# Expert weights by table products: both one-hots from TensorE and ScalarE, shorter lookups on VectorE

## The chip, the cores and the metric

One core of a Trainium2 chip runs the whole kernel. The metric is the device time of one execution in microseconds (us); of several executions the median is given. The core's engines each have an in-order stream of instructions: TensorE (PE, its weight loads PEld), VectorE (DVE), ScalarE (ACT), GpSimd (POOL, which here issues gathers by index), SyncE (SP, which issues the other transfers).

## The reference

One layer of a hybrid encoder over 1024 tokens of width 1024: attention and a long convolution side by side, then a feed-forward part with product keys (PEER), which is where the change lies. For each token and each of 8 heads it finds the 16 best of 128 x 128 experts and sums what they say:

```python
s = jnp.einsum('chpd,hpnd->chpn', q, sub_keys)
sv, si = lax.top_k(s, PEER_TOPK)
cand = sv[:, :, 0, :, None] + sv[:, :, 1, None, :]
cidx = si[:, :, 0, :, None] * PEER_NKEYS + si[:, :, 1, None, :]
...
best, pos = lax.top_k(cand, PEER_TOPK)
eidx = jnp.take_along_axis(cidx, pos, axis=-1)
g = jax.nn.softmax(best, axis=-1)
u = u_tab[eidx]
a = jax.nn.gelu(jnp.einsum('chkd,cd->chk', u, xc), approximate=False)
vv = v_tab[eidx]
return jnp.einsum('chk,chkd->cd', (g * a).astype(vv.dtype), vv)
```

## The kernel before

The 1024 tokens are 8 tiles of 128. Three tiles (NG = 3) are done by gathers: for each of their 128 (head, rank) slots one indirect transfer brings the rows of `peer_u`, and one those of `peer_v`, into `grow` (six buffers), and VectorE takes the dot product (L1244) or adds the weighted row (L1252). The other five (DENSE = 5, 640 tokens) are done by matmuls over all 16384 experts in 128 blocks of 128: `u_part(i)` loads block i of `peer_u` into `ur` (512 KB, one buffer), splits it into a high part `uh` on ScalarE (L291) and a low part `ul` on VectorE (L292), multiplies both with the tokens in two halves of 320 columns (48 matmuls, L285 to L287, into the four banks of `ps_x`) and applies Gelu on ScalarE (L1204). Later the result is weighted with `gt`, the block's column of the table `g_d`, and multiplied with `peer_v`.

The table `g_d` holds for each dense token the weight of every expert; it is what the change makes in another way. For each tile `route` works on VectorE: the best 16 of 128 scores for 16 half-heads (L1019 to L1023), 50 candidate sums a head and their expert numbers (L1039), the best 16 of them (L1045 to L1049), then the look-up of the expert number for each rank: a comparison of the rank's position with 0 to 49, a product with the candidates' numbers, a sum (L1057, L1060, L1061), head by head, 16 ranks x 50 elements each. For a dense tile it then splits the number e into i = e >> 7 and j = e & 127, keeps i as a float, and writes j and j squared in two parts (`jx`) by way of DRAM (`jx_d`, L1093) into `jl` (three loads, L1096), ready to be a matmul's stationary operand. Two transposes on TensorE bring i and the weight w into `ig`.

`build_g` then goes through the tile's 128 tokens, four at a time (32 steps a tile, 160 in all). A step has

```python
nc.tensor.matmul(ps, jl[0:98, c // 32], par_r[0:98, c % 32:c % 32 + NB], start=True, stop=True)
...
nc.vector.tensor_tensor(p1, iota..., ig[:, 0, c:c + NB]..., op=ALU.is_equal)
...
nc.scalar.activation(p2[:, j], ps[:, j], AF.Relu, scale=ig[:, 1, c + j:c + j + 1])
...
nc.tensor.matmul(ps[:, j], p2[:, j], p1[:, j], start=True, stop=True)
```

The first line is a table product: it gives 1 - (j - n) squared for all n from 0 to 127, whose positive part is 1 where n = j and else 0. So `p2` is a one-hot of j, scaled by the weight, made on TensorE and ScalarE; `p1` is a one-hot of i, made by a comparison on VectorE (L1155). The last line multiplies the two for each token (four products), and ScalarE evicts them to `gst` (L1178), which SP writes to `g_d`. Table products run two steps ahead in the two banks of `ps_o`, the one-hots one step ahead.

Order: the first 72 expert blocks (EARLY) are written out beside routing and table building. `weights()` yields an estimated cost at each chunk of route (CHUNK, 14 chunks in all) and at each step of build_g (HOT), and after each 1/71 of the total one `u_part` is written; `tick` likewise paces the gathers. In `weights()` every second step of build_g is followed by one chunk of the next tile's route. From this order a list scheduler of the language lays down each engine's stream before the run, so an instruction can stand before others written ahead of it.

## Time and profile before

| | |
|---|---|
| median of 3 runs | 3322.92 us (3304.04 to 3323.4) |
| the profiled execution | 3313.74 us, span 3312.0 us, mean granted clock 0.958 |
| TensorE busy | 2999.0 us, 91% of the span |
| VectorE busy | 2782.6 us, 84% |
| ScalarE busy | 1254.5 us, 38% |
| GpSimd busy | 1052.3 us, 32% |
| bytes moved | 828.88 MB, mean 250 GB/s |

Busy time is time in which an engine has an instruction under way; matmuls overlap and their ends are modelled, so a busy TensorE isn't one at its peak. Shares are means over stages with different limits, so a change is read in its own stage. The granted clock is TensorE's; 1 is full speed.

### The profile page before, as it was taken

How to read it: one execution, taken by the hardware profiler on the slowest of the kernel's cores; microseconds unless marked ns; L12 is line 12 of the kernel's file. 1: busy time of each engine (PE TensorE's matmuls, PEld its weight loads, DVE VectorE, ACT ScalarE, POOL GpSimd, SP SyncE). 2: the span in 40 equal slices, each digit the busy share in tenths (PEclk: the TensorE clock that was granted, in tenths of full speed). 3: DMA queues.
4: the chain of work that ended last, by engine and by line, in shares of the span. 5: the costliest groups of instructions: out<-in, count | busy, mean ns of one | idle time of the engine just before them, and what ended most of it. 6: DMA issues, size and time to landing. Idle time of an engine off the chain costs nothing.

```text
span 3312.0 us, 44979 instructions
## 1 busy us (share of the span) xinstructions
PE 2999.0 (91%) x15582; PEld 2558.2 (77%) x15582; DVE 2782.6 (84%) x5610; ACT 1254.5 (38%) x2454; POOL 1052.3 (32%) x797
## 2 busy tenths in 40 slices
PE   6999888889999678888989979998999999899997
PEld 4676666655799677788878978886788888688886
DVE  7556899787747999899999978888788888888886
ACT  4544334556333114464555622222222222222222
POOL 0000000000000343334235445555555555555540
PEclk9999999989999899999999989999999999999998
DMA  5344743321454777778778899999899999999993
GB/s 171 103 147 149 236 117 99 99 71 51 160 174 147 259 271 247 267 284 301 273 257 320 327 309 344 331 348 342 310 341 335 354 325 322 346 347 346 330 338 111
DMA packets 355065, 828.88 MB, mean 250 GB/s; under 512 B 34345, under 2 KB 144851, under 8 KB 351253
## 3 DMA queue, kind: packets, MB, share of 16 engines
q1 hardware_dynamic: 243957, 422.25, 38.0%
q0 software_dynamic: 110592, 402.70, 33.9%
q8 instruction: 123, 2.02, 0.2%
q10 hardware_dynamic: 288, 1.05, 0.1%
q14 instruction: 105, 0.86, 0.1%
HBM read 715.52 MB, written 110.33 MB: 249 GB/s over the span
## 4 chain that ended last, share of the span: by engine, by line
PE 36%; DVE 15%; DMA 13%; issue 4%; ACT 2%; SPq 1%; POOL 1%; DVEq 0%; ACTq 0%; POOLq 0%
PE ps_x L285 6%; PE ps_x L287 6%; PE ps_x L286 6%; DMA vr<-in_peer_v 5%; DMA ur<-in_peer_uT 4%; DVE grow L1244 3%; PE ps_h L287 3%; PE ps_h L285 3%; PE ps_h L286 3%; PE ps_h L1177 3%; DVE gacc L1252 2%; PE ps_o L285 2%; PE ps_o L286 2%; PE ps_o L287 2%; DMA grow<-in_peer_u,eid 2%
## 5 line engine op out<-in xcount | busy, mean ns | idle before, releaser
L1231 POOL DMA_INDIRECT grow<-in_peer_v,eid x384 | 516.8, 1346 | 645.2 <-DVE gacc L1252 337.7
L1231 POOL DMA_INDIRECT grow<-in_peer_u,eid x384 | 522.0, 1359 | 560.7 <-DVE grow L1244 211.2
L1252 DVE SCALAR_TENSOR_TENSOR gacc<-grow,dot,gacc 128x1024 f32<-128x1024 f32 x381 | 487.3, 1279 | 6.9 <-DMA grow<-in_peer_v,eid 4.2
L1244 DVE SCALAR_TENSOR_TENSOR grow<-grow,gh 128x1024 f32<-128x1024 f32 x384 | 460.7, 1217 | 15.2 <-DMA grow<-in_peer_u,eid 15.0
L287 PE MATMUL ps_x<-hd,ul 128*128 128x320 f32 x1152 | 371.7, 331 | 54.7 <-DVE ul L292 54.4
L285 PE MATMUL ps_x<-hd,uh 128*128 128x320 f32 x1152 | 377.3, 328 | 39.0 <-ACT uh L291 38.9
L286 PE MATMUL ps_x<-hd,uh 128*128 128x320 f32 x1152 | 373.1, 325 | 0.0
L286 PE MATMUL ps_x<-vl,wh 128*128 128x512 f32 x864 | 341.5, 395 | 7.0 <-DVE vl L292 7.0
L287 PE MATMUL ps_x<-vh,wl 128*128 128x512 f32 x864 | 337.0, 393 | 0.0
L285 PE MATMUL ps_x<-vh,wh 128*128 128x512 f32 x864 | 306.4, 397 | 12.5 <-ACT vh L291 9.6
L291 ACT CAST vh<-vr 128x512 fp32r<-128x512 f32 x256 | 157.3, 619 | 414.8 <-DMA vr<-in_peer_v 304.7
L285 PE MATMUL ps_h<-hd,uh 128*128 128x320 f32 x896 | 279.5, 312 | 20.9 <-ACT uh L291 16.8
L287 PE MATMUL ps_h<-hd,ul 128*128 128x320 f32 x896 | 276.5, 312 | 2.7 <-DVE ul L292 2.6
L286 PE MATMUL ps_h<-hd,uh 128*128 128x320 f32 x896 | 278.6, 311 | 0.0
L287 PEld LDWEIGHTS ps_x<-hd,ul 128*128 128x128 f32 x1152 | 224.3, 197 | 67.8 <-DVE ul L292 62.9
L285 PEld LDWEIGHTS ps_x<-hd,uh 128*128 128x128 f32 x1152 | 227.4, 197 | 45.7 <-ACT uh L291 44.0
L291 ACT CAST uh<-ur 128x1024 fp32r<-128x1024 f32 x128 | 134.9, 1054 | 319.1 <-DMA ur<-in_peer_uT 231.3
L292 DVE TENSOR_TENSOR vl<-vr,vh 128x512 fp32r<-128x512 f32 x256 | 174.5, 686 | 94.8 <-ACT vh L291 94.6
L286 PEld LDWEIGHTS ps_x<-hd,uh 128*128 128x128 f32 x1152 | 227.2, 197 | 1.1
L285 PEld LDWEIGHTS ps_x<-vh,wh 128*128 128x128 f32 x864 | 163.2, 191 | 47.7 <-ACT vh L291 11.7
L1161 ACT ACTIVATE p<-ps_o,ig 128x128 f32<-128x128 f32 x640 | 185.4, 403 | 35.3 <-PE ps_o L1148 35.2
L286 PEld LDWEIGHTS ps_x<-vl,wh 128*128 128x128 f32 x864 | 164.8, 191 | 42.1 <-DVE vl L292 9.4
(363 smaller groups left out, 6904.3 us busy)
## 6 DMA issues: line engine op xcount, KB each, us to landing
ur<-in_peer_uT SPq DMA_DIRECT2D x128, 512.0 KB
vr<-in_peer_v SPq DMA_DIRECT2D x256, 256.0 KB
g_d<-gst SPq DMA_DIRECT2D x20, 2048.0 KB
gt<-g_d SPq DMA_DIRECT2D x32, 1280.0 KB
a_d<-A SPq DMA_DIRECT2D x72, 320.0 KB
A<-a_d SPq DMA_DIRECT2D x72, 320.0 KB
fw<-in_dft_fw SPq DMA_DIRECT2D x64, 256.0 KB
wr<-in_w_in SPq DMA_DIRECT2D x16, 512.0 KB
```

The lines of the kernel that those rows point to most:

```text
L285: nc.tensor.matmul(out, L[0], R[0], start=start, stop=False)
L286: nc.tensor.matmul(out, L[0], R[1], start=False, stop=False)
L287: nc.tensor.matmul(out, L[1], R[0], start=False, stop=stop)
L291: nc.scalar.copy(hi, src)
L292: return nc.vector.tensor_sub(lo, src, hi)
L1161: nc.scalar.activation(p2[:, j], ps[:, j], AF.Relu, scale=ig[:, 1, c + j:c + j + 1])
L1177: nc.tensor.matmul(ps[:, j], p2[:, j], p1[:, j], start=True, stop=True)
L1231: nc_i = nc.gpsimd.indirect_dma_start(out=t, out_offset=None, in_=a["peer_" + kind], in_offset=bass.IndirectOffsetOnAxis(ap=eid[g][:, k:k ...
L1244: nc.vector.scalar_tensor_tensor(t, t, 1.0, h_t, op0=ALU.mult, op1=ALU.mult, accum_out=d[:, k - k0:k - k0 + 1])
L1252: nc.vector.scalar_tensor_tensor(acc, t, dots[k0][:, k - k0:k - k0 + 1], acc, op0=ALU.mult, op1=ALU.add)
```

## The change

The one-hot of i is made as that of j is. `route` writes i, j and their squares, each square in two parts, as six rows (`xb`, through `x_d`) and loads them with six transfers into a `jl` with a slot for i and one for j; only the weight is still transposed. `parabola` does two table products a step, that for i into a bank of `ps_x`, that for j into `ps_o` as before; `hots` takes the positive part of the first with one activation over four tokens (128x512), in place of the comparison.

The candidates are put in another order, so that those that can have rank 0 to 3 are the first 16 and those that can have rank 4 to 7 are within the first 32. The look-up then goes by ranks: ranks 0 to 3 of all heads over 16 candidates, ranks 4 to 7 over 32, ranks 8 to 15 over 50 in two halves of the heads: four groups of three instructions with 512, 1024, 1600 and 1600 elements, where there were eight groups of 800. The constants of the order follow (12 chunks of route, three of five steps of build_g followed by one).

```diff
@@ -1003,10 +1003,14 @@
 
     NEG = -3.0e38
     NCAND = 50
-    rows = [(0, 1, 16), (1, 1, 8), (2, 1, 5), (3, 1, 4), (4, 1, 3), (5, 3, 2), (8, 8, 1)]
+    blocks = [(0, 4, 0, 4), (0, 2, 4, 4), (4, 4, 0, 2), (0, 1, 8, 8), (8, 8, 0, 1), (2, 1, 4, 1), (4, 1, 2, 1)]
+    finds = [(0, 8, 0, 4, 16), (0, 8, 4, 8, 32), (0, 4, 8, 16, NCAND), (4, 8, 8, 16, NCAND)]
 
     routed = []
-    CHUNK = 62.0 / 14
+    CHUNK = 55.0 / 12
 
     def route(tt, rp, done):
 
@@ -1032,10 +1036,10 @@
         nc.vector.tensor_scalar(sf4[:, :, 0], sf4[:, :, 0], 128.0, None, op0=ALU.mult)
         for eng, dst, src in ((nc.vector, cand, sv4), (nc.vector, cidx, sf4)):
             off = 0
-            for a0, na, nb in rows:
+            for a0, na, b0, nb in blocks:
                 o = dst[:, :, off:off + na * nb].rearrange("p h (x y) -> p h x y", y=nb)
                 x = src[:, :, 0, a0:a0 + na].unsqueeze(3).to_broadcast([P, 8, na, nb])
-                y = src[:, :, 1, 0:nb].unsqueeze(2).to_broadcast([P, 8, na, nb])
+                y = src[:, :, 1, b0:b0 + nb].unsqueeze(2).to_broadcast([P, 8, na, nb])
                 eng.tensor_add(o, x, y)
                 off += na * nb
             assert off == NCAND
@@ -1052,15 +1056,16 @@
         pf = rp.tile([P, 8, 16], F32, name="r_pf")
         nc.vector.tensor_copy(pf, pos)
         ef = rp.tile([P, 8, 16], F32, name="r_ef")
-        for h in range(8):
-            oh = rp.tile([P, 16, NCAND], F32, name="r_oh")
+        for h0, h1, k0, k1, n in finds:
+            nh, nk = h1 - h0, k1 - k0
+            oh = rp.tile([P, 32 * NCAND], F32, name="r_oh")[:, 0:nh * nk * n]
+            oh = oh.rearrange("p (h k n) -> p h k n", h=nh, k=nk)
             nc.vector.tensor_tensor(
-                oh, iota[:, 0:NCAND].unsqueeze(1).to_broadcast([P, 16, NCAND]),
-                pf[:, h].unsqueeze(2).to_broadcast([P, 16, NCAND]), op=ALU.is_equal)
-            nc.vector.tensor_mul(oh, oh, cidx[:, h:h + 1].to_broadcast([P, 16, NCAND]))
-            nc.vector.reduce_sum(ef[:, h], oh, axis=AX.X)
-            if h % 2:
-                yield 1.5 * CHUNK
+                oh, iota[:, 0:n].unsqueeze(1).unsqueeze(1).to_broadcast([P, nh, nk, n]),
+                pf[:, h0:h1, k0:k1].unsqueeze(3).to_broadcast([P, nh, nk, n]), op=ALU.is_equal)
+            nc.vector.tensor_mul(oh, oh, cidx[:, h0:h1, 0:n].unsqueeze(2).to_broadcast([P, nh, nk, n]))
+            nc.vector.reduce_sum(ef[:, h0:h1, k0:k1], oh, axis=AX.X)
+            yield CHUNK
         w = rp.tile([P, 8, 16], F32, name="r_w")
         nc.vector.tensor_sub(w, best, best[:, :, 0:1].to_broadcast([P, 8, 16]))
         nc.scalar.activation(w, w, AF.Exp)
@@ -1077,27 +1082,23 @@
         nc.vector.tensor_mul(w, w, den_b)
         ei = rp.tile([P, P], I32, name="r_ei")
         nc.vector.tensor_copy(ei, ef2)
-        ij = rp.tile([P, 2, P], I32, name="r_ij")
-        nc.vector.tensor_scalar(ij[:, 0], ei, 7, None, op0=ALU.arith_shift_right)
-        nc.vector.tensor_scalar(ij[:, 1], ei, 127, None, op0=ALU.bitwise_and)
-        ijf = rp.tile([P, P], F32, name="r_ijf")
-        nc.vector.tensor_copy(ijf, ij[:, 0])
-        jj = rp.tile([P, P], I32, name="r_jj")
-        nc.vector.tensor_tensor(jj, ij[:, 1], ij[:, 1], op=ALU.mult)
-        jp = rp.tile([P, 2, P], I32, name="r_jp")
-        nc.vector.tensor_scalar(jp[:, 1], jj, 127, None, op0=ALU.bitwise_and)
-        nc.vector.tensor_scalar(jp[:, 0], jj, 127 << 7, None, op0=ALU.bitwise_and)
-        jx = rp.tile([P, 3, P], BF16, name="r_jx")
-        nc.vector.tensor_copy(jx[:, 0], ij[:, 1])
-        nc.vector.tensor_copy(jx[:, 1:3], jp)
-        nc.sync.dma_start(jx_d[tt].rearrange("r t s -> t r s"), jx)
+        xx = rp.tile([P, 3, 2, P], I32, name="r_xx")
+        nc.vector.tensor_scalar(xx[:, 0, 0], ei, 7, None, op0=ALU.arith_shift_right)
+        nc.vector.tensor_scalar(xx[:, 0, 1], ei, 127, None, op0=ALU.bitwise_and)
+        x2 = rp.tile([P, 2, P], I32, name="r_x2")
+        nc.vector.tensor_tensor(x2, xx[:, 0], xx[:, 0], op=ALU.mult)
+        nc.vector.tensor_scalar(xx[:, 1], x2, 127 << 7, None, op0=ALU.bitwise_and)
+        nc.vector.tensor_scalar(xx[:, 2], x2, 127, None, op0=ALU.bitwise_and)
+        xb = rp.tile([P, 6, P], BF16, name="r_xb")
+        nc.vector.tensor_copy(xb, xx.rearrange("p r w s -> p (r w) s"))
+        nc.sync.dma_start(x_d[tt].rearrange("r t s -> t r s"), xb)
         jl = jls[tt % 2]
-        for r in range(3):
-            nc.sync.dma_start(jl[32 * r:32 * r + 32], jx_d[tt, r].rearrange("(q t) s -> t q s", t=32))
-        ps = psO.tile([P, 2, P], F32, name="ps_o0")
-        nc.tensor.transpose(ps[:, 0], ijf, ident)
-        nc.tensor.transpose(ps[:, 1], w.rearrange("p h k -> p (h k)"), ident)
-        ig = rp.tile([P, 2, P], F32, name="ig", bufs=2)
+        for r in range(6):
+            nc.sync.dma_start(jl[32 * (r // 2):32 * (r // 2) + 32, r % 2],
+                              x_d[tt, r].rearrange("(q t) s -> t q s", t=32))
+        ps = psO.tile([P, P], F32, name="ps_o0")
+        nc.tensor.transpose(ps, w.rearrange("p h k -> p (h k)"), ident)
+        ig = rp.tile([P, P], F32, name="ig", bufs=2)
         nc.scalar.copy(ig, ps)
         done.append((ig, jl))
         yield CHUNK
@@ -1129,7 +1130,7 @@
     CS = 32
     GI = 4
     NCS = TD // CS
-    jx_d = dram.tile([NT, 3, P, P], BF16, name="jx_d")
+    x_d = dram.tile([NT, 6, P, P], BF16, name="x_d")
     NB = 4
     HOT = 0.69
     g_d = dram.tile([NCS, P, P, CS], F32, name="g_d")
@@ -1143,22 +1144,22 @@
 
         def parabola(n):
             cs, c4 = steps[n]
-            ps = psO.tile([P, NB, P], F32, name=f"ps_o{n % 2}")
             c = cs * CS + c4
-            nc.tensor.matmul(ps, jl[0:98, c // 32], par_r[0:98, c % 32:c % 32 + NB], start=True, stop=True)
-            par[n] = ps
+            par[n] = []
+            for w in range(2):
+                ps = psO.tile([P, NB, P], F32, name=f"ps_o{n % 2}") if w else psX.tile([P, NB, P], F32, name="ps_x")
+                nc.tensor.matmul(ps, jl[0:98, w, c // 32], par_r[0:98, c % 32:c % 32 + NB], start=True, stop=True)
+                par[n].append(ps)
 
         def hots(n):
             cs, c4 = steps[n]
             c = cs * CS + c4
             p1 = gp.tile([P, NB, P], F32, name="p1", bufs=4)
-            nc.vector.tensor_tensor(p1, iota.unsqueeze(1).to_broadcast([P, NB, P]),
-                                    ig[:, 0, c:c + NB].unsqueeze(2).to_broadcast([P, NB, P]),
-                                    op=ALU.is_equal)
             p2 = gp.tile([P, NB, P], F32, name="p2", bufs=4)
-            ps = par.pop(n)
+            pi, pj = par.pop(n)
+            nc.scalar.activation(p1, pi, AF.Relu)
             for j in range(NB):
-                nc.scalar.activation(p2[:, j], ps[:, j], AF.Relu, scale=ig[:, 1, c + j:c + j + 1])
+                nc.scalar.activation(p2[:, j], pj[:, j], AF.Relu, scale=ig[:, c + j:c + j + 1])
             hot[n] = p1, p2
 
         parabola(0)
@@ -1293,7 +1294,7 @@
         par_r = gp.tile([98, 32, P], BF16, name="par_r")
         nc.vector.tensor_mul(par_r, base.unsqueeze(1).to_broadcast([98, 32, P]),
                              own.unsqueeze(2).to_broadcast([98, 32, P]))
-        jls = [gp.tile([98, 4, P], BF16, name=f"jl{i}") for i in range(2)]
+        jls = [gp.tile([98, 2, 4, P], BF16, name=f"jl{i}") for i in range(2)]
         for jl in jls:
             nc.gpsimd.memset(jl[96:98], 1.0)
         r0 = route(0, rp, [])
@@ -1315,14 +1316,14 @@
                 beside = route(NG + t + 1, rp, done) if t + 1 < DENSE else route(1, rp, done)
                 for n, c in enumerate(build_g(done[t], t, gp)):
                     yield c
-                    if n % 2 == 0:
+                    if n % 5 in (0, 2, 4):
                         yield next(beside, 0.0)
                 yield from beside
             for g in range(2, NG):
                 yield from route(g, rp, done)
 
         gw = weights()
-        total = (NT - 1) * 14 * CHUNK + TD // NB * HOT
+        total = (NT - 1) * 12 * CHUNK + TD // NB * HOT
         done = 0.0
         for e in range(EARLY):
             while done < (e + 1) * total / GFILL:
```

## Rows read from the trace of the kernel before

**Rows 1.** Busy us of each engine in four stretches (PEclk: granted clock, full speed 1).
```profile
core 0: us, PE busy (x) PEld busy (x) DVE busy (x) ACT busy (x) POOL busy (x), PEclk, DMA share, GB/s
...
1071.00:1288.00 217.00, 154.50 (x935) 147.86 (x934) 212.65 (x795) 40.16 (x66) 90.30 (x67) 0.90 0.75 261
1288.00:1890.00 602.00, 540.14 (x3699) 514.04 (x3698) 565.36 (x1475) 352.80 (x965) 229.39 (x167) 0.96 0.81 286
1890.00:1951.00 61.00, 50.36 (x284) 48.25 (x284) 58.15 (x65) 11.56 (x19) 33.42 (x24) 0.86 0.88 314
1951.00:3312.00 1361.00, 1284.50 (x6441) 1112.90 (x6440) 1150.49 (x1564) 352.36 (x582) 682.44 (x508) 0.97 0.91 324
```

**Rows 2.** Instructions on tile ur, 1068 to 1952 us: ns min/median/max, first and last start.
```profile
L1193 SPq DMA_DIRECT2D ur<-in_peer_uT x73: 332/333/15352, 1068.5 to 1951.0; - x73
L291 ACT CAST uh<-ur x72: 1027/1051/1190, 1078.5 to 1947.6; 128x1024 fp32r<-128x1024 f32 x72
L292 DVE TENSOR_TENSOR ul<-ur,uh x73: 1194/1217/1236, 1067.2 to 1948.7; 128x1024 fp32r<-128x1024 f32 x73
```

**Rows 3.** Timeline of SP, ScalarE and VectorE, first link: start us, us.
```profile
1068.46 0.33 SPq L1193 DMA_DIRECT2D ur<-in_peer_uT  x1
...
1078.49 1.05 ACT L291 CAST uh<-ur 128x1024 fp32r<-128x1024 f32 x1 [1.21 <-DMA ur<-in_peer_uT]
...
1092.27 1.20 DVE L292 TENSOR_TENSOR ul<-ur,uh 128x1024 fp32r<-128x1024 f32 x1
```

**Rows 4.** Who waited for whom, 1071 to 1951 us: us, times, longest.
```profile
ACT uh L291 <- DMA ur<-in_peer_uT: 223.9, 44, 19.2
...
PE ps_x L287 <- DVE ul L292: 54.4, 26, 12.6
...
PE ps_o L1148 <- DMA jl<-jx_d: 26.3, 5, 8.6
```

**Rows 5.** VectorE's groups by line and shape, 1071 to 1951 us.
```profile
L1155 DVE TENSOR_TENSOR p<-iota,ig 128x512 f32<-128x512 f32 x160 | 107.4, 683 | 15.7 <-PE ps_h L1177 15.5
...
L292 DVE TENSOR_TENSOR ul<-ur,uh 128x1024 fp32r<-128x1024 f32 x72 | 87.5, 1215 | 15.9 <-ACT uh L291 15.8
...
L1057 DVE TENSOR_TENSOR r_oh<-iota,r_pf 128x800 f32<-128x800 f32 x56 | 55.0, 982 | 0.0
...
L1092 DVE CAST r_jx<-r_jp 128x256 bf16<-128x256 int32 x5 | 1.6, 310 | 0.0
...
L1039 DVE TENSOR_TENSOR r_cidx<-r_sf 128x24 f32<-128x24 f32 x7 | 1.2, 176 | 0.0
```

**Rows 6.** Instructions on tile ur, 1952 to 3312 us.
```profile
L291 ACT CAST uh<-ur x53: 1037/1049/1057, 1971.9 to 3177.4; 128x1024 fp32r<-128x1024 f32 x53
...
L292 DVE TENSOR_TENSOR ul<-ur,uh x53: 1207/1219/1228, 1973.3 to 3178.4; 128x1024 fp32r<-128x1024 f32 x53
```

**Rows 7.** ScalarE's groups by line and shape, 1071 to 1951 us.
```profile
L1178 ACT COPY gst<-ps_h 128x512 f32<-128x512 f32 x160 | 97.7, 616 | 38.3 <-PE ps_h L1177 38.1
```

**Rows 8.** Timeline of TensorE, 1592 to 1596 us: start us, us.
```profile
1591.64 0.38 PE L1148 MATMUL ps_o<-par_r,jl 98*128 98x512 bf16 x1
1591.67 0.50 PE L287 MATMUL ps_x<-hd,ul 128*128 128x320 f32 x1
1592.01 0.30 PE L285 MATMUL ps_x<-hd,uh 128*128 128x320 f32 x1
...
1593.47 0.31 PE L286 MATMUL ps_x<-hd,uh 128*128 128x320 f32 x1
1593.62 1.05 PE L1177 MATMUL ps_h<-p,p 128*128 128x128 f32 x8
1594.51 0.38 PE L1148 MATMUL ps_o<-par_r,jl 98*128 98x512 bf16 x1
```

**Rows 9.** Waits of SP's queue, and the loads of jl, about 1068 to 1952 us.
```profile
SPq L1096 <- DMA jx_d<-r_jx: 21.3, 5, 6.6
...
L1096 SPq DMA_DIRECT2D jl<-jx_d x15: 318/424/1467, 1282.7 to 1801.4; - x15
```

## The prediction

> **What bounds the kernel now.** I read the stretches first [rows 1]. Everything that the diff touches runs before 1951 us, and nearly all of it between 1071 and 1951 us, where routing, the building of the weight tables, 72 expert blocks (u_part) and a share of the gathers stand side by side. The reader is to see that VectorE is the fullest engine there: 212.65 + 565.36 + 58.15 = 836 us of 880, 95%; TensorE shows 745 us, ScalarE 405 us, and the DMA share is 0.75 to 0.88. After 1951 us TensorE shows 1284 of 1361 us, with nothing of the change in it, so I take that part (and the part before 1071 us, but for one route) as it is.
>
> A full engine isn't yet the path. Second, the tile ur, one buffer deep [rows 2]: from the issue at 1068.5 to that at 1951.0 us there are 72 links of load, ScalarE's cast uh, VectorE's subtraction ul, next issue. No link overlaps the next, so their sum is the stage: 882 us, 12.2 us a link. The first link [rows 3] shows its pieces: issue 1068.46, cast 1078.49 (1.05 us), subtraction only at 1092.27 (1.20 us), though ur and uh were ready at 1079.5: VectorE was at routing and gathers. Added up so over all 72 links from the starts and ends that the timeline gives: issue to cast 538 us, cast 76, cast's end to subtraction 154, subtraction 88, subtraction to next issue 26. So VectorE's queue is worth 154 us here, 2.13 us a link; the largest piece, 538 us, is the load with what stands ahead of the cast on ScalarE. Third, the waits [rows 4]: ScalarE stands 223.9 us for ur to land, TensorE's idle time goes to uh and ul, and the first table product of each tile waits 26.3 us in all for jl. All of these are the same chain, seen from the waiting side.
>
> **The change, part by part.** The sum is made against the profiled execution: span 3312.0 us, 3313.7 us with 1.7 around it; that is 9 us under the median of the runs (3322.92) and inside their 3304 to 3323.
>
> *VectorE, one-hot.* The comparison p1 goes: 160 x 683 ns = 109 us (107.4 as a union) [rows 5], all inside the stage.
>
> *VectorE, lookups.* Before, 24 instructions of 800 elements a route at 0.98 us: 23.5 us. After, three passes over 512, 1024, 1600 and 1600 elements. Rows: 512 elements 683 ns, 1024 elements 1215 ns [rows 5], so 1.04 ns an element, and 1600 elements by that line 1813 ns (an estimate; the row of 800, 982 ns, lies on it). 683 + 1215 + 2 x 1813 = 5.52 us a pass, 16.6 us a route, 7.0 us less; seven routes in the stage, 49 us, and 7 us for route 0 ahead of it. Bounds: if the longer broadcast patterns cost a fifth more, 26 us of 49 are left; nothing in the rows suggests below the line.
>
> *VectorE, the rest.* The candidate sums stay at 14 instructions and 400 elements a table: two 8-element ones (no dearer than the 24-element 176 ns [rows 5]) and 64-element ones take the place of lengths between; nothing. The tail of a dense route has ten instructions before and eight after, some twice or six times as long: by the 256-element cast of 310 ns [rows 5], six times 128 elements is 0.7 us, the whole within 0.5 us a tile. I take +1 us in all.
>
> VectorE so falls from 836 to 836 - 107 - 49 + 1 = 681 us. What that is worth is read from the chain, not from the sum: only the 154 us of waiting can go, and not all. In the last stretch the same two instructions of 53 links [rows 6] stand 74.5 us apart in all (added up likewise), 1.41 us a link, with VectorE at 1150/1361 = 0.845. Against 2.13 at 0.95, the line falls 0.69 us for each 0.1; at 681 of some 835 us, 0.815, it gives 1.2 us. 72 x (2.13 - 1.2) = **67 us off**. Ends: 0 (the order of the queue, not its fullness, makes the wait) and 154 (no wait left).
>
> *ScalarE.* One positive part of 128x512 out of PSUM a step is added. The nearest row is the eviction gst of the same size, 616 ns, 97.7 us as a union of 160 [rows 7]; so +98 us, 405 to 503 of some 835. It is covered only where ScalarE would else stand idle (475 us now, half of it for ur itself). In two cases of five, 28 of 72 links, the cast didn't wait for ur (in 44 it did [rows 4]), so ScalarE already has something ahead of it; I let a tenth of the new work stand before a cast: **+10 us**. Ends: 0 and 98.
>
> By the Trainium skill, page ScalarE: Activation LUTs, section Rules for kernel authors, a relu belongs on VectorE, which speaks against this move. This case's rows have it the other way at this size in f32, 683 ns on VectorE against 616 on ScalarE; with the positive part kept on VectorE only the 49 us of lookups would leave it, and by the line above some 17 us of the 67 would be left, the sum near 3310 us.
>
> *TensorE.* 160 more table products of 98x512. The row shows 0.38 us, but ends are modelled; starts tell more [rows 8]: matmuls of an expert block follow each other at 0.146 us (ten from 1592.01 to 1593.47); from a table product at 1591.64 past one such matmul to the next it is 0.37, so 0.22 us for the product, 35 us in all. Eight halves of the four products of a step take 0.89 us (1593.62 to 1594.51). At such spacings the stage holds 72 x 48 x 0.146 + 160 x 0.89 + 160 x 0.22 = 682 us of work, after the change 717. Under 835 us that is 86%, and the last stretch runs at more, so I cost it at 0 on the path. Ends: 0 and 35. Five fewer transposes are nothing.
>
> *PSUM.* The product for p1 takes its bank from ps_x, which the expert blocks fill too: two of four banks may be held by p1's products when two steps are in flight. I take 0; see the rivals.
>
> *SP's queue.* Per tile one store of six rows instead of three, then six loads of jl for three; the loads wait for the store, and issues of ur queue behind them. Before: 21.3 us of such waiting over five tiles, loads of 0.42 us each [rows 9]. 5 x 3 x 0.42 = 6 us of issue, and a store with twice the packets between 0 and 4 us later each. Most of it meets an ur that has been issued already: **+5 us**, ends 0 and 27.
>
> *DMA.* The bytes stay; in a stage 5% shorter the loads meet denser gathers. 538 us of load, of which the share in contention grows: **+10 us**, ends 0 and 30.
>
> *Order.* Routing's interleave (19 slots in 32 steps instead of 16, 12 yields as before) ends a tile's route three or four steps before; that moves jl forward, where the first product waits 5 us a tile [rows 4]. TensorE isn't the chain: 0, at best 26. Route 0's 7 us lies before the first gather, beside the scores: -2.
>
> Sum: -67 + 10 + 5 + 10 - 2 = -44. 3313.7 - 44 = 3270 us; the stage ends at 837 instead of 880.
>
> **The rivals.**
> (a) *VectorE was the stage, no single link.* Then the stage follows its work, 681 us at the 0.845 that it reaches in the last stretch: 806 us, 74 off, 3240 us. For it: 95% busy, gathers and casts both behind it. Against: 538 us of the chain are load, and the DMA share would be 0.80 x 880 / 806 = 0.87.
> (b) *The middle stretch is full already.* TensorE shows 540 of 602 us there; with 35 more and 94%, as in the last stretch, it needs 612. Then only the ends, without table building, gain: VectorE at 212.65 of 217 us loses 11 us, at 58.15 of 61 loses 7. 18 off, 3296 us. For it: [rows 1]. Against: the starts [rows 8] say 86%, not 90.
> (c) *The shared banks, slower.* ScalarE is served in order, and at 44 casts it stands 5.1 us for ur. An expert block's first half that needs the bank of a Gelu or of a p1 product queued behind such a cast stops TensorE, which is in order too, and with it the next tables. Price: up to 5.1 us, 47 of the 72 blocks in the middle stretch; if half of them pay 3.5 us it costs 82, 38 over the sum: 3352 us. It decides from 13 blocks on (13 x 3.5 = 44), beyond which the change loses. For it: ScalarE's cast stands ahead of a Gelu at times; four banks for two uses. Against: p1's product is read in the very next steps.
> That the change doesn't do what it says isn't likely: p1 leaves VectorE whole.
>
> **How the numbers follow.** Runs of this kernel differ by 19 us in 3320, so 1% is what can be told from no change. Forecast 0.48, (a) 0.17, (b) 0.24, (c) 0.11. The forecast's own ends (chain wait 30 to 100 us off, costs 0 to 50) reach from about 3235 to 3300. For 8 in 10 I cut the fastest tenth of (a) and most of (c): 3228 to 3325. Under 3290 (1% below the median) lie (a) and most of the forecast: faster 0.60; (b), the forecast's upper end and the mild half of (c) are within 1%: 0.31; slower 0.09.
>
> **What the profile after would show.** VectorE near 680 us before the last ur of the stage, its share about 0.81; lookups of 1.8 us; cast's end to subtraction 1.2 us a link instead of 2.1; that last issue near 1907 us instead of 1951. ScalarE with 160 more rows of about 0.6 us. If issue to cast grows by more than 20 us, ScalarE or the DMA engines took the gain; if TensorE waits for ScalarE's Gelu or p1 ahead of ps_x, it is (c). Wrong would be the forecast if the subtraction's wait came from the order of VectorE's queue, which a program lays down ahead, or if gathers used the freed time to run ahead and filled the DMA engines.

## The result and the profile after

The change made the kernel slower: a median of 3364.03 us (3351.33 to 3372.21, four runs) against 3322.56 us of four runs of the kernel before, ratio 1.0128, 95% interval 1.0096 to 1.0161. The profiled execution took 3362.37 us, its span 3360.6 us. Beside the experiments below, the kernel before had medians of 3298.55 to 3305.68 us, so what follows is compared by ratios, each against runs of the kernel before taken beside it.

The stretches of the kernel after, read as [rows 1] (a TensorE stall cut out by itself):

```profile
1069.00:1149.00 80.00, 45.41 (x275) 43.28 (x273) 75.43 (x344) 15.67 (x24) 33.09 (x29) 0.81 0.80 292
1149.00:1240.00 91.00, 12.53 (x74) 11.38 (x74) 89.44 (x321) 8.95 (x23) 39.64 (x29) 0.55 0.59 192
1240.00:1931.00 691.00, 626.45 (x4208) 574.75 (x4207) 528.26 (x1409) 438.66 (x1135) 263.34 (x201) 0.96 0.79 287
1931.00:2005.00 74.00, 74.00 (x507) 74.00 (x506) 12.81 (x11) 19.92 (x33) 0.00 (x0) 1.00 0.47 162
2005.00:3361.00 1356.00, 1285.85 (x6470) 1114.38 (x6468) 1151.83 (x1560) 350.61 (x580) 679.21 (x508) 0.98 0.92 324
```

VectorE got its relief: 75 + 89 + 528 + 13 = 706 us where it had 836. The last stretch is as it was, 1356 us from 2005 us on for 1361 from 1951. The whole loss lies in the stage between, where the last issue of ur comes at 2017.3 instead of 1951.0 us [rows 2]:

```profile
L1194 SPq DMA_DIRECT2D ur<-in_peer_uT x73: 332/333/1365, 1069.1 to 2017.3; - x73
L291 ACT CAST uh<-ur x72: 1027/1047/1267, 1078.9 to 2003.4; 128x1024 fp32r<-128x1024 f32 x72
```

The waits of the stage (compare [rows 4]) name the place, one wait of 84.1 us in which TensorE stands before a tile's first table product:

```profile
DVE ul L292 <- ACT uh L291: 199.6, 32, 22.2
...
PE ps_x L1151 <- DMA jl<-x_d: 84.1, 1, 84.1
...
ACT r_w L1071 <- DVE r_w L1070: 74.1, 5, 62.2
...
ACT uh L291 <- DMA ur<-in_peer_uT: 67.5, 21, 17.7
...
PE ps_x L1151 <- ACT p L1160: 2.6, 2, 2.3
```

Its timeline, rows of VectorE, SP, ScalarE and TensorE in the order of their starts:

```profile
1142.88 0.48 PE L1100 MATMUL ps_o<-ident,r_w 128*128 128x128 f32 x1 [9.73 <-DVE r_w L1082]
...
1143.44 1.04 ACT L291 CAST uh<-ur 128x1024 fp32r<-128x1024 f32 x1 [8.89 <-DMA ur<-in_peer_uT]
...
1208.19 0.31 ACT L1071 ACTIVATE r_w<-r_w 128x128 f32<-128x128 f32 x1 [62.24 <-DVE r_w L1070]
...
1219.07 0.54 DVE L1093 CAST r_xb<-r_xx 128x768 bf16<-128x768 int32 x1
...
1219.63 0.38 SPq L1094 DMA_DIRECT2D x_d<-r_xb  x1
1222.20 2.70 SPq L1097 DMA_DIRECT2D jl<-x_d  x6
...
1227.47 1.44 PE L1151 MATMUL ps_x<-par_r,jl 98*128 98x512 bf16 x3 [84.11 <-DMA jl<-x_d]
...
1228.10 1.58 ACT L1160 ACTIVATE p<-ps_x 128x512 f32<-128x512 f32 x3 [18.07 <-PE ps_x L1151]
...
1228.35 0.83 PE L285 MATMUL ps_x<-hd,uh 128*128 128x320 f32 x1
...
1238.57 1.05 ACT L291 CAST uh<-ur 128x1024 fp32r<-128x1024 f32 x1
```

Read it backwards. The product at 1227.47 needs jl; jl is loaded at 1222.20, after the store at 1219.63, after VectorE's cast xb at 1219.07. VectorE isn't idle meanwhile (89.44 of 91 us): it works through gathers and two tiles' routes and only then reaches the tail of the first. But the product stands in TensorE's stream right behind the transpose at 1142.88, and TensorE takes its stream in order, so it does nothing for 84 us: two expert blocks were cast at 1133.52 and 1143.44, their matmuls stand behind the product, and the first of them starts at 1228.35; ScalarE stands 62.24 us before the Exp of the next route and 18.07 us before the first positive part. The expert block whose ur was issued at 1149.6 gets its cast at 1238.57: one link of 89 us. Counting the matmuls of expert blocks ahead of the first table product in TensorE's stream shows what moved: 21.1 blocks before, 7.0 after.

The links of ur, added up as in the prediction (us; load is issue to cast, wait is cast's end to subtraction, sub the subtraction, issue its end to the next issue):

```
                 load cast wait sub issue  sum
before            538   76  154  87   27   883
after             648   76  115  88   21   948
```

The sum grows by 66 us and the span by 49. Part of the difference is the last issue, which follows its subtraction after 1.1 us in the kernel before and after 11.6 in the kernel after.

So there are two findings. The load piece holds the stall. And the wait for VectorE fell by 39 us where 67 were forecast, though VectorE's busy time fell nearly as forecast. In 100-us slices, VectorE (third figure after the length) shows where its free time went:

```profile
1471.00:1571.00 100.00, 96.39 (x665) 89.14 (x664) 97.43 (x261) 69.56 (x185) 49.42 (x38) 0.98 0.94 335
1571.00:1671.00 100.00, 83.03 (x551) 75.45 (x550) 80.78 (x162) 60.07 (x155) 55.88 (x40) 0.91 0.87 320
1671.00:1771.00 100.00, 81.66 (x503) 72.77 (x502) 73.41 (x157) 51.50 (x127) 52.01 (x42) 0.90 0.90 339
1771.00:1871.00 100.00, 99.83 (x706) 94.20 (x706) 48.25 (x45) 73.37 (x187) 25.94 (x19) 1.00 0.69 250
1871.00:1971.00 100.00, 98.70 (x683) 93.39 (x682) 13.48 (x11) 54.43 (x136) 0.00 (x0) 1.00 0.42 151
```

VectorE is 95 to 98% full in each slice up to 1571 us and nearly idle at the end of the stage, where GpSimd has no gather left at all. Routes and gathers were pulled ahead: the stage holds 255 of VectorE's gather steps in both kernels, and the third gathered tile's expert numbers are ready at 1790.0 us (the last start below), at 1947.2 in the kernel before.

```profile
L1078 DVE CAST eid<-r_ef x3: 215/220/228, 1048.2 to 1790.0; 128x128 int32<-128x128 f32 x3
```

### The profile page after: what moved, and what is told of

It is laid out like the page before. It is cut to its first block, busy times and chain, and to the rows that moved or that the text cites. A ratio compares the mean times of both kernels' runs of the same rounds, so it can differ in the third digit from the quotient of the medians.

```text
span 3360.6 us, 45130 instructions
## 1 busy us (share of the span) xinstructions
PE 3010.4 (90%) x15737; PEld 2548.6 (76%) x15737; DVE 2645.7 (79%) x5344; ACT 1325.6 (39%) x2610; POOL 1028.4 (31%) x797
## 4 chain that ended last, share of the span: by engine, by line
PE 57%; DVE 20%; DMA 11%; issue 6%; ACT 4%; POOL 2%; SPq 1%; DVEq 0%; ACTq 0%; POOLq 0%
PE ps_x L285 10%; PE ps_x L286 10%; PE ps_x L287 10%; PE ps_h L287 3%; PE ps_h L285 3%; PE ps_h L286 3%; DMA vr<-in_peer_v 3%; PE ps_o L285 3%; DVE gacc L1253 3%; PE ps_o L286 3%; PE ps_o L287 3%; DVE grow L1245 2%; POOL grow L1232 2%; DMA ur<-in_peer_uT 2%; DMA grow<-in_peer_u,eid 2%
## 5 line engine op out<-in xcount | busy, mean ns | idle before, releaser
L1232 POOL DMA_INDIRECT grow<-in_peer_u,eid x384 | 508.6, 1325 | 743.4 <-DVE gacc L334 210.6
L1232 POOL DMA_INDIRECT grow<-in_peer_v,eid x384 | 507.8, 1322 | 529.3 <-DVE gacc L1253 271.2
L285 PE MATMUL ps_x<-hd,uh 128*128 128x320 f32 x1152 | 370.7, 322 | 32.5 <-ACT uh L291 32.3
L287 PE MATMUL ps_x<-hd,ul 128*128 128x320 f32 x1152 | 361.9, 319 | 29.2 <-DVE ul L292 29.0
L286 PE MATMUL ps_x<-hd,uh 128*128 128x320 f32 x1152 | 364.6, 317 | 0.0
L292 DVE TENSOR_TENSOR ul<-ur,uh 128x1024 fp32r<-128x1024 f32 x128 | 156.1, 1219 | 235.9 <-ACT uh L291 234.3
L285 PEld LDWEIGHTS ps_x<-hd,uh 128*128 128x128 f32 x1152 | 222.2, 193 | 47.4 <-ACT uh L291 44.4
L286 PEld LDWEIGHTS ps_x<-hd,uh 128*128 128x128 f32 x1152 | 222.2, 193 | 0.6
```

The lines of the kernel that those rows point to most:

```text
L285: nc.tensor.matmul(out, L[0], R[0], start=start, stop=False)
L286: nc.tensor.matmul(out, L[0], R[1], start=False, stop=False)
L287: nc.tensor.matmul(out, L[1], R[0], start=False, stop=stop)
L292: return nc.vector.tensor_sub(lo, src, hi)
L1232: nc_i = nc.gpsimd.indirect_dma_start(out=t, out_offset=None, in_=a["peer_" + kind], in_offset=bass.IndirectOffsetOnAxis(ap=eid[g][:, k:k ...
```

## The experiments

The theory: the loss is the place of the first table product in TensorE's stream; and no gain appears because work pulled ahead fills VectorE again. Rivals: the positive parts on ScalarE or the extra products cost the time themselves; the lookups' longer patterns do; (c) of the prediction, the shared banks.

**1. The first tile's chunks of route weighed three times**, so that more expert blocks are written out ahead of its tables; nothing else of the change undone.

```diff
+FIRST = 3.0
...
-            yield from route(NG, rp, done)
+            for c in route(NG, rp, done):
+                yield FIRST * c
...
-        total = (NT - 1) * 12 * CHUNK + TD // NB * HOT
+        total = (NT - 2 + FIRST) * 12 * CHUNK + TD // NB * HOT
```

> The changed kernel with one edit: the chunks of the first dense tile's route count three times in the order, so that some 18 expert blocks stand ahead of the first table product in TensorE's stream instead of 7. Theory (order): the changed kernel lost its gain to one stall, 84 us of TensorE and ScalarE ahead of the first table product, which the order laid down too early; then that wait falls below 15 us and the time is 3280 to 3305 us. Rival (new load): the loss lies in the table building itself, with two products and one more activation a step in shared banks; then the stretch only moves and the time stays at 3350 to 3370 us.

Ratio 0.9991 (0.9974 to 1.0008). 18.0 blocks stand ahead, the first product runs at 1249 us, and TensorE stands nowhere over 1.1 us right ahead of a table product. The loss is gone, 1.0128 to 0.9991 or some 45 us for 84 us of stall (VectorE works on during it). But there is no gain: load 531, wait 145 of 879 us. VectorE is full again, and empty late:

```profile
1271.00:1371.00 100.00, 92.53 (x629) 85.64 (x629) 100.00 (x353) 66.12 (x173) 37.46 (x29) 0.97 0.84 297
...
1471.00:1571.00 100.00, 95.73 (x653) 86.75 (x652) 99.09 (x309) 69.24 (x188) 44.45 (x34) 0.98 0.89 317
...
1871.00:1971.00 100.00, 96.96 (x622) 94.15 (x621) 27.80 (x31) 26.78 (x45) 8.19 (x6) 0.97 0.64 220
```

**2. The lookups alone.** The kernel after with its one-hot part put back to the comparison:

```diff
-            nc.scalar.activation(p1, pi, AF.Relu)
+            nc.vector.tensor_tensor(p1, iota.unsqueeze(1).to_broadcast([P, NB, P]),
+                                    ig[:, 0, c:c + NB].unsqueeze(2).to_broadcast([P, NB, P]),
+                                    op=ALU.is_equal)
```

(and with it the tail of route, jl and parabola as before).

> The new candidate order and shorter lookups alone (with their constants of the order); the one-hot of i by comparison on VectorE as before. Theory (order): 15.5 blocks stand ahead of the first table product, between the 7 of the changed kernel and the 21 of the one before, so a stall of 10 to 40 us; the seven us a route of VectorE are gained: 3300 to 3325 us. Rival (new load): no new load, so the whole gain of the lookups, 3295 to 3305 us, with no stall.

0.9986 (0.9969 to 1.0003): no loss, no gain. 15.5 blocks ahead, and the expected stall of 10 to 40 us didn't come: 1.8 us at most. The wait for VectorE is 184 us, more than before, so the lookups' relief isn't seen in it either.

**3. The one-hot part alone**, in the kernel before (the same lines the other way round, eight lookups of 800 elements kept).

> The one-hot of i from a table product and a positive part alone; lookups, candidate order and constants as before. Theory (order): 8 blocks stand ahead of the first table product, so the stall is there as in the changed kernel or longer, since VectorE's lookups ahead of it are the long ones: 85 to 110 us, time 3360 to 3390 us. Rival (new load): slower too, but by the stretch of table building: its 72 links would show more time between issue and cast outside the one stall.

1.0271 (1.0243 to 1.0299), worse than the whole change. 8.0 blocks ahead, and a stall of 126.4 us; the second fence is a slice within it, TensorE at nothing and VectorE at 100:

```profile
PE ps_x L1146 <- DMA jl<-x_d: 126.7, 2, 126.4
```

```profile
1171.00:1271.00 100.00, 0.00 (x0) 0.00 (x0) 100.00 (x392) 1.81 (x3) 48.34 (x36) 0.50 0.61 202
```

The early place comes with the one-hot part, and the stall is longer than the 110 us expected at most: VectorE has more to do before the first tail here. The price grows with the stall.

**4. Gathers paced ahead**, on experiment 1: if VectorE has time to spare, use it.

```diff
-EHEAD = 0.28
+EHEAD = 0.36
```

> As e1_first3, and a larger share of the gather steps (0.36 for 0.28) written beside the first 72 blocks. In the changed kernel GpSimd and the DMA engines stand idle in the last 74 us of that stage, as the next group of gathers is written later. Theory (order): the gathers fill that end and fewer are left for the last stage: 5 to 20 us below e1_first3. Rival: the last stage is bound by TensorE, so nothing is won there, and VectorE has more to do in the first: the same as e1_first3 or slower by up to 15 us.

1.0143 (1.0119 to 1.0167), a miss. 335 of the gathers' VectorE steps fell into the stage instead of 255, and the wait rose from 145 to 198 us. (Its expectation calls GpSimd and the DMA engines idle in the last 74 us of the changed kernel's stage; GpSimd is, the DMA share is 0.47.) It was the first sign that VectorE's freed time isn't free where the casts wait.

**5 to 8. Gathers held.** Each expert block's gathers may be laid down only behind that block's subtraction:

```diff
-        split(nc, uh, ul, ur)
+        uls.append(split(nc, uh, ul, ur))
...
-            tick(UC)
+            with tc.issue_after(uls[-1].ins):
+                tick(UC)
```

On experiment 1:

> As e1_first3, and the gathers' instructions on VectorE held behind the subtraction of the expert block they are written with. Theory (spent ahead): VectorE's freed time was used by later routes and gathers that the order pulls forward, so VectorE stays at 97 to 100% until 1570 us and idles at the end, and the wait from cast to subtraction stays near 2 us; with the gathers held it falls and the stage ends 20 to 50 us earlier, ratio to the kernel before 0.985 to 0.995. Rival (new load): what is left is the cost of ScalarE's and TensorE's added work; holding the gathers changes nothing, ratio 0.997 to 1.005.

On the kernel after, without the weight of three:

> The changed kernel with the gathers held in the same way, and no change to the route's place. Theory (order): some ten pairs of gather steps fewer stand ahead of the first tile's table rows on VectorE, at 2.5 us a pair, so the stall ahead of the first table product is 55 to 70 us instead of 84, and the time 15 to 30 us below the changed kernel, ratio 1.003 to 1.009. Rival: the stall isn't on the path, as VectorE is full in it; the time is that of the changed kernel, ratio 1.011 to 1.016.

On the kernel before:

> Control: the kernel before with its gathers held in the same way as in e5_held, nothing of the change. Theory (spent ahead): VectorE has no time to spare there, so holding moves nothing, ratio 0.995 to 1.005. Rival: holding is what helps, whatever the kernel, ratio below 0.99.

Experiment 5: 0.9868 (0.983 to 0.9907), wait 94 us, stage 838. Experiment 6: 1.0009 (0.9985 to 1.0032), wait 81 us, but with a stall of its own, 60.6 us, which again stands ahead of the first table product:

```profile
PE ps_x L1151 <- DMA jl<-x_d: 60.6, 1, 60.6
```

The kernel before with the hold: 0.9918 (0.9889 to 0.9947). That was expected to do nothing and did something, so part of what experiment 5 won is the hold's and not the change's. Its wait stayed at 151 us; the load piece fell to 476, and no run shows why. Behind the stage TensorE waits once for 45.2 us there.

The hold does a second thing: fewer gather steps fall into the stage, 230 in experiments 5 and 6 and 225 in the kernel before with the hold, where it was 255. In experiment 4, 80 steps more made the stage 60 us longer, 0.75 us a step; by that estimate the 25 steps fewer are worth some 19 of the 41 us by which experiment 5's stage is shorter than experiment 1's. The stretch behind the stage doesn't pay for them (1343.6 us, 1342.5 in experiment 1). No run holds the gathers and keeps their number, so the two aren't told apart here.

**Routes held as well**, on experiment 5:

```diff
-                c = next(gw, None)
+                with (tc.issue_after(uls[-1].ins) if uls else ExitStack()):
+                    c = next(gw, None)
```

> As e5_held, and the chunks of route and the table building held behind the subtraction of the block before as well, so that VectorE follows the written order. Theory (spent ahead): the wait from cast to subtraction falls below 1 us a link, ratio 0.975 to 0.99. Rival (new load): 0.997 to 1.01; or the held order leaves VectorE idle and the route of the first tile late, above 1.01.

0.978 (0.9747 to 0.9812), the best version of all. With 222 gather steps in the stage for 230, the 32 us that this step takes off the stage are the order's but for some 6, by the same estimate. The wait is 32 us, 0.45 us a link; the last issue of ur comes at 1874.4, the stage takes 806 us. VectorE stands at an even 81 to 88% from 1271 to 1771 us, and TensorE is now full:

```profile
1271.00:1371.00 100.00, 98.64 (x692) 91.41 (x693) 82.13 (x247) 80.81 (x217) 27.12 (x24) 1.00 0.84 296
1371.00:1471.00 100.00, 99.74 (x703) 92.49 (x702) 82.44 (x240) 79.70 (x213) 34.78 (x28) 1.00 0.84 301
...
1671.00:1771.00 100.00, 98.71 (x690) 90.44 (x689) 81.86 (x267) 77.75 (x209) 32.24 (x24) 1.00 0.80 290
```

**9, 10. Both holds on the kernel after (no weight of three), and on the kernel before (with it, over 14 chunks).**

> The changed kernel with gathers, route and table building held, and the first route counted once, so that again 7 blocks stand ahead of the first table product. Theory (order): a stall of 40 to 60 us stays ahead of the first table product, and the time lies 25 to 55 us above e7_bothheld, ratio 0.987 to 0.995. Rival: the early start of the tables is no harm in itself, within 10 us of e7_bothheld.

> Control of e7_bothheld: the kernel before with the same three edits of the order (first route counted three times, gathers and route held behind their blocks), nothing of the change. Theory (the change pays once the order leaves VectorE's freed time where the casts wait): VectorE has 156 us more to do and is full, so the stage is VectorE's, ratio to the kernel before 0.988 to 1.0, and the change is worth 1 to 2% between the two. Rival (the order alone): the same 0.975 to 0.982 as e7_bothheld.

The first: 0.9888 (0.9849 to 0.9926). Wait 35 us as in the best version, 7.0 blocks ahead and a stall of 32.4 us; the stage is 832 against 806 us. So the place of the first table product alone is worth 1.1%, some 36 us, here too, with a stall shorter than the 40 to 60 us expected. The second: 1.0058 (1.0037 to 1.008), outside both ranges, but it is a poor control: its routing ends at 1943 us, behind the last issue of ur at 1885.9, and there TensorE waits once for 69.9 us. Of the other kernels only the one before with its gathers held has such a wait, the 45.2 us above; its routing ends behind the stage too, at 1929 us for 1896.7:

```profile
PE ps_h L286 <- ACT A L1205: 70.2, 2, 69.9
```

**11 to 13. The suspected costs doubled or moved, in the best version.** The product for i issued twice; its positive part done twice; its positive part on VectorE.

```diff
-                nc.tensor.matmul(ps, jl[0:98, w, c // 32], par_r[...], start=True, stop=True)
+                for _ in range(1 if w else 2):
+                    nc.tensor.matmul(ps, jl[0:98, w, c // 32], par_r[...], start=True, stop=True)
```

```diff
             nc.scalar.activation(p1, pi, AF.Relu)
+            nc.scalar.activation(p1, pi, AF.Relu)
```

```diff
-            nc.scalar.activation(p1, pi, AF.Relu)
+            nc.vector.tensor_scalar(p1, pi, 0.0, None, op0=ALU.max)
```

> As e7_bothheld, with the table product for i done twice in each step (160 more of 0.22 us on TensorE, same result). TensorE shows 98 to 100% between 1271 and 1771 us there. Theory (TensorE is the bound once the order is held): 25 to 45 us above e7_bothheld. Rival (ScalarE or the transfers are the bound): within 10 us of it.

> As e7_bothheld, with the positive part for p1 done twice in each step (160 more of 0.6 us on ScalarE, 98 us, same result). Theory (TensorE is the bound): within 15 us of e7_bothheld, ScalarE's work lies beside. Rival (ScalarE's queue is in the chain, cast by cast): 30 to 98 us above it.

> As e7_bothheld, with the positive part for p1 taken on VectorE out of PSUM instead of ScalarE (160 of some 0.7 us, VectorE from 83% to some 95%, ScalarE 98 us less). Theory (VectorE's queue is what the casts wait for): 30 to 70 us above e7_bothheld. Rival (ScalarE's queue is the dearer one, as the doubled activation cost 76 us): at or below e7_bothheld.

Product twice: 0.9912 (0.9881 to 0.9944), 1.3% or some 44 us over the best version for 35 us of products (160 x 0.22 [rows 8]); the stage grew by 35 us, the load piece from 583 to 623. Positive part twice: 1.0011 (0.9991 to 1.0031), 2.3% or some 76 us, 65 of them in the stage, where ScalarE's busy time went from 479 to 553 us; load 651. That ScalarE had room for it was a miss. On VectorE: 0.9996 (0.9978 to 1.0014), 2.2% or some 71 us; the wait rose to 55 and the load to 608. Only 37 us of that are the stage's: between the two profiled executions some 42 us lie behind the last issue of ur, and no run shows why. Groups of VectorE in that kernel (the form of [rows 5]), then a slice:

```profile
L1161 DVE TENSOR_SCALAR p<-ps_x 128x512 f32<-128x512 f32 x160 | 104.9, 680 | 54.7 <-PE ps_x L1152 54.7
```

```profile
1271.00:1371.00 100.00, 83.14 (x571) 77.10 (x570) 89.73 (x266) 53.19 (x143) 27.70 (x24) 0.92 0.81 283
```

The positive part costs VectorE what the comparison did, and VectorE stands 54.7 us in front of it for the product, a wait that the subtractions behind it in the queue share; TensorE falls from 98.64 to 83.14 of this slice.

**14. The lookups alone, in the order of the best version** (experiment 2 with the weight of three and both holds).

> As e7_bothheld, but with the one-hot of i by comparison on VectorE as in the kernel before: the lookups alone, in the held order. Theory (the one-hot's move frees VectorE where it is the bound): VectorE has 107 us more, near 97% of the stage, ratio to the kernel before 0.988 to 1.0, so the one-hot is worth 1 to 2% in the held order. Rival (its new work on ScalarE and TensorE costs what it frees): within 0.4% of e7_bothheld, 0.974 to 0.982.

0.9812 (0.9776 to 0.9847) against 0.978 (0.9747 to 0.9812): the one-hot part is worth 0.3% here, which the intervals don't tell from nothing. The theory's 1 to 2% didn't come; the rival's range holds the result. Stage 804 us, wait 148, load 461; VectorE is full and TensorE less so:

```profile
1371.00:1471.00 100.00, 92.96 (x667) 88.90 (x666) 100.00 (x300) 66.06 (x184) 33.92 (x27) 1.00 0.83 307
```

The one-hot part trades 116 us of waiting for VectorE (148 against 32) for 122 us of load (583 against 461), the piece in which the cast waits for the transfer and for what stands ahead of it on ScalarE. All runs together (links in us; blocks: expert blocks ahead of the first table product; stall: TensorE's longest idle time right ahead of any table product):

```
                     load cast wait sub issue  sum  blocks  stall  ratio
before                538   76  154  87   27   883   21.1    8.6   1
after                 648   76  115  88   21   948    7.0   84.1   1.0128
1 first tile x3       531   78  145  87   38   879   18.0    1.1   0.9991
2 lookups alone       500   76  184  88   31   878   15.5    1.8   0.9986
3 one-hots alone      687   77   82  88   29   963    8.0  126.4   1.0271
4 = 1 + gathers early 554   77  198  87   22   938   18.1    1.9   1.0143
5 = 1 + gathers held  552   77   94  88   28   838   19.0    2.9   0.9868
6 after + gathers h.  605   77   81  88   30   879    7.0   60.6   1.0009
before + gathers held 476   76  151  87   31   822   22.6    2.4   0.9918
7 = 5 + routes held   583   75   32  88   28   806   19.0   16.9   0.978
after + both held     605   76   35  88   29   832    7.0   32.4   0.9888
before + x3 + both    508   76  127  88   17   815   21.1    2.1   1.0058
7 + product twice     623   75   27  88   28   841   19.0   17.0   0.9912
7 + relu twice        651   76   29  88   28   872   19.0   17.3   1.0011
7 + relu on VectorE   608   76   55  88   17   844   19.0   17.2   0.9996
14 lookups, as 7      461   76  148  88   30   804   20.8    0.5   0.9812
```

## Why the prediction was wrong

**The step that failed** is the term *Order*: "TensorE isn't the chain: 0, at best 26". It took the route's earlier end for a gain and never asked where the first table product would stand against the blocks ahead of it. It stands 14 blocks earlier, and an 84.1 us stall of TensorE and ScalarE came of it, worth about 45 us (experiment 1 against the kernel after). The kernels with 7.0 or 8.0 blocks ahead all stall (32.4 to 126.4 us), those with 15.5 to 22.6 don't or by 17 us. Where it is written says more. The constants that pace the order put the first table product behind 8 written blocks in the kernel before (a first route of 62 over 544.4 / 71 a block), behind 7 in the kernel after (55 over 495.4 / 71), and behind 19 with the weight of three. In every kernel with a product for i it runs within one block of that place (7.0, 8.0, 18.0 to 19.0). In the five that make the one-hot of i by comparison it runs later than that, at 15.5 to 22.6. So the change hardly wrote the product earlier; it kept it from slipping 13 blocks back. A likely reason is that the product for i takes its bank from `ps_x`, in turn with the expert blocks written behind it, but no run here gives it another bank, so that part stays open.

**A second term was mis-sized**: -67 for the wait of VectorE. It measured -39 in the kernel after and -9 with the stall removed (145 of 154). The line through two stages (2.13 us at 0.95, 1.41 at 0.845) held VectorE's share for the cause. Experiments 1 and 5 have the same share, 0.805 of the stage (707 of 879 us, 675 of 838), and waits of 145 and 94 us: what counts is what stands ahead of the subtraction in the queue, as the prediction's last paragraph allowed. Routes and gathers ran ahead into the freed time; with both held back the wait falls to 0.45 us a link at a share of 0.81 to 0.88 in most slices, far below that line's 1.2.

**The work itself was sized well.** Comparisons gone, lookups of 512, 1024 and 1600 elements at 680, 1216 and 1816 ns (forecast 683, 1215, 1813), products of the stage in these groups of the kernel after:

```profile
L1066 DVE TENSOR_TENSOR r_oh<-r_oh,r_cidx 128x1600 f32<-128x1600 f32 x14 | 25.4, 1816 | 0.0
...
L1066 DVE TENSOR_TENSOR r_oh<-r_oh,r_cidx 128x1024 f32<-128x1024 f32 x7 | 8.5, 1216 | 0.0
...
L1066 DVE TENSOR_TENSOR r_oh<-r_oh,r_cidx 128x512 f32<-128x512 f32 x7 | 4.8, 680 | 0.0
```

VectorE went to 706 and not 681 us; the last section says where most of the 25 come from.

**ScalarE** was given 98 us; its busy time rose by 79, from 405 to 483 us. The rows' 658 and 616 ns say more than an instruction adds, since their records overlap (last section):

```profile
L1160 ACT ACTIVATE p<-ps_x 128x512 f32<-128x512 f32 x160 | 100.9, 658 | 33.6 <-PE ps_x L1151 32.3 <-issue 1.2
```

Its term of +10 was too small wherever the order lets the chain run: the load piece of the best version is 122 us over experiment 14's, which has neither the positive parts nor the products for i; a second positive part adds 74 us to ScalarE's busy time and costs 76 us, 65 of them in the stage, within the term's own ends of 0 and 98, where the forecast let a tenth of the work count. **TensorE** at 0 has the same fault: with both held it shows 98 to 100% for most of 500 us, and 35 us more cost 44, 35 of them in the stage. That is what rival (b) said of the middle stretch, once nothing else held the stage up. Rival (a)'s stage of 806 us is the one that the best version reached, but with TensorE full and VectorE not.

**SP and DMA** (+5, +10): not seen. Subtraction to next issue, without the last issue, is 26 us before, 10 after and 25 in experiment 1, and in experiment 1 the load piece is 531 for 538. Route 0's -2 isn't seen either: the stage's first issue of ur is at 1069.1 us for 1068.5. **The banks**, rival (c) (its 3352 us is 82 over the sum, 38 over the kernel before), had the right sign, but not by the wait it names: TensorE's product for i waits 2.6 us in all for p1's reads, and the expert blocks' matmuls for a Gelu's bank in no wait of 1.9 us or more in sum. Whether the shared banks set the product's place is the open part above.

By the Trainium skill, page ScalarE: Activation LUTs, section Rules for kernel authors, a relu belongs on VectorE; the reason it gives is VectorE's speed in bf16. At 128x512 in f32 out of PSUM this case doesn't bear the rule out: 658 ns on ScalarE, 680 on VectorE, and the kernel 2.2% slower with it there. The prediction's own figure for that variant, some 40 us worse than the forecast, had the right sign and was too mild (71 us, in the best version's order).

## What to carry to other kernels

Time freed on a full engine is worth something only where a chain waits for that engine; background work can move up in its queue and take that time, so hold such work behind the chain's own instruction before you count the gain. When a change moves the first use of a table to an in-order engine, look in the laid-down stream how much independent work stands ahead of it, and compare that with when its producer can be done. A row's mean duration isn't what an instruction adds to a full engine: take the distance between starts. Two changes sold as one should be run apart in the order that suits them: here the lookups and the holds carry nearly all of 0.978.

## What was not expected of the hardware

A removed instruction on VectorE is worth less than its duration when its neighbours follow closely: in the kernel before the comparison that starts at 1559.91 us lasts 0.68 us, but the next instruction starts 0.60 us after it. Counted so, from each start to the next one's, the 160 comparisons took 97 us where the forecast took off 107, and the lookups gave back 43 us and not 49. That is 16 of the 25 us that VectorE's busy time is above the forecast.

ScalarE's instructions of one shape got longer as more of them were there: the eviction gst of 128x512 took 616 ns in the kernel before [rows 7], 651 after, 732 with the positive part done twice. The traces tell what grew: the overlap with the instruction in front. Where ScalarE was idle before it, an eviction takes 587 ns in all three kernels (55, 32 and 8 of the 160), and beyond the end of the instruction in front of it one adds 518, 499 and 482 ns on the mean.

After the stall TensorE ran slowly at first: matmuls of the block started 0.27 us apart from 1228.98 to 1231.38 us and 0.15 us apart from there; the granted clock is 0.50, the lower of its two levels (1.2 GHz), from 1150 to 1227 us, where TensorE does nothing, and from 1228.9 to 1231.3, and 1.00 from 1232 to 1236. By those spacings the stall's end costs about 1 us, nothing beside the stall.
